# A mixture of experts with its up-projections turned round: weights stationary, 96 token slots streaming

## The chip, the cores and the metric

The kernel runs on one core of one Trainium2 chip. The metric is the device time of one execution in microseconds, given as the median of several runs. TensorE (PE) multiplies a stationary operand, which a weight load (PEld) brings in, with a moving operand that streams through it column by column; results go to PSUM. VectorE (DVE), ScalarE (ACT) and GpSimd (POOL) work beside it, and 16 DMA engines move data from HBM, issued here by SyncE's queue (SP). TensorE's granted clock has two levels, 1.2 and 2.4 GHz; the profile gives it as a share of the upper one.

## What is computed

Two decoder layers over 256 tokens of 1024 channels. Each has a mixer (attention and a short convolution), a feed-forward part and a gated embedding. The feed-forward part is dense in layer 0 and routed in layer 1, which is the part that the change is about:

```python
def moe_swiglu(x, router_w, w1, w3, w2):
    xt = x.reshape(bsz * s_len, d)                       # 256 x 1024
    logits = (xt @ router_w).astype(jnp.float32)         # 8 experts
    top_vals, top_idx = lax.top_k(logits, TOP_K)         # 2 of them for each token
    gates = jax.nn.softmax(top_vals, axis=-1)
    ...
    for e in range(N_EXPERTS):
        out = out + combine[:, e:e + 1] * swiglu(xt, w1[e], w3[e], w2[e])

def swiglu(x, w1, w3, w2):
    return (jax.nn.silu(x @ w1) * (x @ w3)) @ w2         # 1024 -> 3584 -> 1024
```

Its input is `rmsnorm(h, ffn_norm_g)`: h times one factor for each token and one gain for each channel.

## The kernel before

**Precision.** Every large product is made of values in two parts, high and low, both rounded to the type fp32r: x = xh + xl, w = wh + wl. `mm3` (lines 180 to 183) issues three matmuls for each product: low x times high w, high x times low w, and high times high. The weights arrive in fp32; `split` (line 87) makes wh with a ScalarE cast (line 94) and wl with a VectorE subtraction (line 95), in parts of 1024 columns. `plan` lists all weight halves in the order of their use; `weights` and `prepare` keep five split parts (`NPART`) ahead of TensorE, and `loads` keeps the transfers ahead of that.

**Order.** In the routed layer the instructions of TensorE, ScalarE and VectorE run in the order in which the code is written. There is no planner.

**Routing.** `Moe.route` transposes h, makes the router's logits (`logits`, line 717, matmuls of 8 columns), and `choose` ranks them on VectorE, counts each token's slot within its expert with small matmuls (line 746 to 750) and leaves in `pos` the slot of each token. `Gather` builds for a pair of experts a one-hot matrix `sl` of tokens to slots, 128 slots for each expert, and its `step` multiplies the split h (`Parts`, tile `hx`) with it: the result, tile `pg`, holds the tokens of the two experts with channels on the partitions, and `scaled_split` applies the channel gain and makes the two parts of it. The token factor (1/rms) is not yet in it: `slots` brings it to each slot with one-column matmuls (line 820) as `rslot`, together with the transposed matrix `slT` for the way back. An expert that has more than 128 tokens is served by a second pass over all weights (`over`), behind a branch at the end.

**Experts.** Eight experts follow one another, each in 7 blocks of 512 hidden units. `expert_up` makes a block's two up-projections (tile `pe`, one PSUM bank each): the gathered tokens are stationary, 128 slots wide, and the weights stream, 512 columns a matmul; 8 channel blocks times 3 matmuls for each of w1 and w3. Silu with the factor `rslot` (line 843) and the product (line 846) give m with slots on the partitions. `hidden_T` (line 578) transposes m with four matmuls against the identity (line 581) and splits it into `th` and `tl`, which `expert_down` uses as the stationary operand, one block later, against streaming columns of w2 (tile `y`, two banks). `main` writes the order of a block: the four half up-projections, half of the down-projection of the block before, `hidden_T`, the other half. At an expert's end `y_split` and `combine` bring the sums back to the tokens.

The lines of the profile are those of the code below.

Of the kernel before, what the change touches and what calls it, by code (L numbers as in the profile page):

```python
# [16 lines left out]
P = 128  # L17
# [21 lines left out]
# columns of the constant pack  # L39
# [5 lines left out]
def trunk(ctx: ExitStack, tc: tile.TileContext, a, out):  # L45
# [13 lines left out]
    # ---- parameters and constants  # L59
# [11 lines left out]
    onesr = const.tile([P, P], F32R, name="onesr")  # L71
    one1 = const.tile([P, 1], F32, name="one1")
# [7 lines left out]
    # ---- building blocks  # L80
# [52 lines left out]
    def loads(upto):  # L133
        """parts up to that one, loaded"""
# [8 lines left out]
    def prepare(upto, eng=nc.vector):  # L143
        """parts up to that one, split"""
# [45 lines left out]
    class TokenRstd:  # L190
        """1 / rms of each token of h, [P, NT]: part(n) for each half of the channels, then done()"""
# [21 lines left out]
    def x_tiles(raw=False):  # L213
        """two parts of a transposed input; of two that live at a time, one is raw: in weights' slots"""
        return [rawp.tile([P, KD, S], F32R, tag="raw", name=n) if raw else xp.tile([P, KD, S], F32R, tag=n, name=n)
                for n in ("xh", "xl")]

    class Transposed:
        """gain * h over channels, in two parts, and the token factors; step(k) does channels k, k + 1 of 128"""
# [6 lines left out]
        def step(self, k):  # L226
            # a bank for each channel block, so that two engines read at a time
# [78 lines left out]
    # ---- the mixer: attention and short convolution  # L306
    def mixer(l, xt, after):
        """xt: transposed input, whose steps 4 and 6 are still to do where l > 0; after: makes the next one"""
        with tc.tile_pool(name="att", bufs=2) as ap, tc.tile_pool(name="att1", bufs=1) as a1:
# [29 lines left out]
            def v_g():  # L339
                """the values over tokens, and the convolution's input"""  # L340
# [17 lines left out]
            def consts():  # L358
                # of 0 and 1, so the rounding keeps them
# [839 lines left out]
```

## Time and profile before

| | |
|---|---|
| time, median of 3 runs | 1545.15 us (1544.93 to 1545.29) |
| span of the profiled execution | 1541.0 us |
| TensorE busy | 1521.9 us (99%) |
| VectorE busy | 1282.6 us (83%) |
| ScalarE busy | 1096.0 us (71%) |
| chain that ended last | 97% TensorE |
| read from HBM | 443.4 MB, 288 GB/s over the span |
| the experts' stretch | about 522 to 1507 us |

The span is that of one execution under the profiler; the median of the runs is 4.15 us more. Busy time of TensorE is the time in which at least one matmul is under way. A matmul's own duration holds its latency, and matmuls overlap, so the durations of a group add up to more than the time they take; the distance from one start to the next tells the pace. The pages below name a group of instructions by line, engine, operation and "output<-inputs".

### The profile page before, as it was taken

The numbers are of one execution on the slowest core, as the hardware profiler recorded it, in microseconds if no ns is written. First come the engines' busy times: TensorE is split into PE (matmuls) and PEld (weight loads), VectorE is DVE, ScalarE is ACT, GpSimd is POOL, SyncE is SP. The second block draws the span as 40 slices with busy tenths as digits, with TensorE's granted clock in tenths as the row PEclk, the third lists the DMA queues.
The fourth block names the chain that finished last, engine by engine and source line by source line (L and its number), as shares of the span: only waits on it lengthen the run. The fifth ranks groups of instructions, "written<-read, shape, count | busy, mean of one in ns | idle before, by whom it ended". The sixth has DMA issues, their size and how long they took to land.

```text
span 1541.0 us, 19945 instructions
## 1 busy us (share of the span) xinstructions
PE 1521.9 (99%) x7249; PEld 1261.5 (82%) x7249; DVE 1282.6 (83%) x1553; ACT 1096.0 (71%) x1470; POOL 92.7 (6%) x96
## 2 busy tenths in 40 slices
PE   7999999999999999999999999999999999999998
PEld 6888888887888788888888888888888888888886
DVE  7886555556788799899899999999999999999895
ACT  5756444446675687878777778787787887877874
POOL 3430000000243000000000000000000000000000
PEclk9999999999999899999999999999999999999999
DMA  9656554343435699897999998999998899999960
GB/s 359 251 197 241 191 186 176 137 162 111 169 148 203 236 379 371 313 349 288 360 372 375 351 361 328 375 408 378 353 360 331 313 362 368 377 343 338 362 259 30
DMA packets 64043, 445.84 MB, mean 289 GB/s; under 512 B 7104, under 2 KB 9024, under 8 KB 10432
## 3 DMA queue, kind: packets, MB, share of 16 engines
q1 hardware_dynamic: 63936, 444.48, 75.8%
q8 instruction: 59, 0.97, 0.2%
q14 instruction: 48, 0.39, 0.1%
HBM read 443.40 MB, written 1.05 MB: 288 GB/s over the span
## 4 chain that ended last, share of the span: by engine, by line
PE 97%; DVE 1%; DMA 0%; ACT 0%; issue 0%; SPq 0%; POOL 0%; DVEq 0%; ACTq 0%
PE pe L181 13%; PE pe L183 13%; PE pe L182 13%; PE y L183 8%; PE y L182 8%; PE y L181 8%; PE p L183 3%; PE p L182 3%; PE p L181 3%; PE pt L581 2%; PE pu L181 2%; PE pu L182 1%; PE pu L183 1%; PE pj L181 1%; PE pj L183 1%; PE pj L182 1%
## 5 line engine op out<-in xcount | busy, mean ns | idle before, releaser
L95 DVE TENSOR_TENSOR wl<-raw,wh 128x1024 fp32r<-128x1024 f32 (+1 forms) x999 | 1017.6, 1058 | 178.8 <-ACT wh L94 167.3
L94 ACT CAST wh<-raw 128x1024 fp32r<-128x1024 f32 (+1 forms) x1000 | 881.4, 913 | 242.8 <-PE pe L183 78.9
L181 PE MATMUL pe<-wh,xl 128*128 128x512 f32 x896 | 350.6, 391 | 0.0
L183 PE MATMUL pe<-wh,xh 128*128 128x512 f32 x896 | 349.2, 390 | 0.0
L182 PE MATMUL pe<-wl,xh 128*128 128x512 f32 x896 | 348.6, 389 | 0.0
L181 PE MATMUL y<-wh,tl 128*128 128x512 f32 x560 | 226.2, 404 | 0.0
L182 PE MATMUL y<-wl,th 128*128 128x512 f32 x560 | 220.8, 394 | 0.5 <-DVE wl L95 0.5
L183 PE MATMUL y<-wh,th 128*128 128x512 f32 x560 | 220.9, 395 | 0.0
L183 PEld LDWEIGHTS pe<-wh,xh 128*128 128x128 f32 x896 | 168.1, 188 | 36.2
L182 PEld LDWEIGHTS pe<-wl,xh 128*128 128x128 f32 x896 | 168.3, 188 | 35.9 <-DVE wl L95 0.4
L181 PEld LDWEIGHTS pe<-wh,xl 128*128 128x128 f32 x896 | 168.2, 188 | 35.1
L183 PEld LDWEIGHTS y<-wh,th 128*128 128x128 f32 x560 | 105.1, 188 | 25.2
L182 PEld LDWEIGHTS y<-wl,th 128*128 128x128 f32 x560 | 105.3, 188 | 22.7 <-DVE wl L95 1.2
L181 PEld LDWEIGHTS y<-wh,tl 128*128 128x128 f32 x560 | 105.3, 188 | 21.6 <-ACT wh L94 0.2
L181 PE MATMUL p<-wh,xl 128*128 128x512 f32 x224 | 87.8, 392 | 0.0
L183 PE MATMUL p<-wh,xh 128*128 128x512 f32 x224 | 87.3, 390 | 0.0
L182 PE MATMUL p<-wl,xh 128*128 128x512 f32 x224 | 87.2, 389 | 0.0
L585 ACT CAST th<-pt 128x512 fp32r<-128x512 f32 x70 | 40.9, 586 | 41.7 <-PE pt L581 41.7
L95 POOL TENSOR_TENSOR wl<-raw,wh 128x1024 fp32r<-128x1024 f32 x1 | 2.4, 2372 | 990.8 <-ACT wh L94 990.8
L181 PE MATMUL pu<-xh,wl 128*128 128x256 f32 x192 | 56.4, 294 | 0.0
L182 PE MATMUL pu<-xl,wh 128*128 128x256 f32 x192 | 54.2, 282 | 0.0
L183 PE MATMUL pu<-xh,wh 128*128 128x256 f32 x192 | 54.2, 282 | 0.0
(203 smaller groups left out, 1565.4 us busy)
## 6 DMA issues: line engine op xcount, KB each, us to landing
raw<-m_w SPq DMA_DIRECT2D x336, 1024.0 KB, 5.7
raw<-d_w SPq DMA_DIRECT2D x42, 1024.0 KB, 4.8
raw<-w_in SPq DMA_DIRECT2D x22, 1024.0 KB, 6.9
raw<-w_o SPq DMA_DIRECT2D x8, 1024.0 KB, 6.7
raw<-w_g SPq DMA_DIRECT2D x8, 1024.0 KB, 4.8
raw<-w_p SPq DMA_DIRECT2D x2, 1024.0 KB, 4.8
raw<-w_in SPq DMA_DIRECT2D x4, 256.0 KB, 4.4
raw<-w_in SPq DMA_DIRECT2D x2, 512.0 KB, 8.8
```

The lines of the kernel that those rows point to most:

```text
L94: nc.scalar.copy(wh[:, cs], raw[:, cs])
L95: eng.tensor_sub(wl[:, cs], raw[:, cs], wh[:, cs].bitcast(F32))
L181: nc.tensor.matmul(ps, ll, rh, start=start, stop=False)
L182: nc.tensor.matmul(ps, lh, rl, start=False, stop=False)
L183: nc.tensor.matmul(ps, lh, rh, start=False, stop=stop)
L581: nc.tensor.transpose(pt[:, c * P:(c + 1) * P], m[:, c * P:(c + 1) * P], ident)
L585: nc.scalar.copy(th, pv)
```

## The change

- A new constant `CAP = 96` is the number of slots of an expert in a pass. The one-hot matrices, the gathered tokens and the down-projection's stationary operand have 96 slots in place of 128. The branch to the further passes is taken when an expert has more than 96 tokens.
- The gathered tokens are kept as `[channel block, expert, high and low, slot]` in one tile (`Gather.x`).
- `expert_up` has the weights as the stationary operand, 128 hidden columns at a time, and streams the tokens: for each channel block and each of four column blocks q, one matmul of wl with the 96 high slots, and one of wh with the 192 high and low slots, whose low half goes to other columns of the same PSUM bank. An up-projection now has two banks, each with two q's.
- After the last channel block ScalarE copies the low sums to SBUF (tile `lo`), and `fold` adds them to the high sums with an identity matmul. Then come Silu and the product. The result already has hidden units on the partitions, so `hidden_T` isn't called in the experts; `fold(1)` splits it into `th` and `tl`.
- The token factors go into the split of h: `Parts.part` uses `scaled_split` with the factor of each token, which `Route.factors` makes before the choice. Silu and the product have no factor any more, and `slots` no one-column matmuls.
- PSUM: `pe` goes to the four banks of `acc`, `y` to the two of `mm`, the embedding's sums to `tp`. xh and xl of the other stages lie in one tile, `x`. Comments and docstrings are taken out.

```diff
+CAP = 96
 ...
 class Parts:
-            nc.scalar.copy(hh, hn)
-            nc.vector.tensor_sub(hl, hn, hh.bitcast(F32))
+            scaled_split(hh, hl, hn, self.r()[:, t:t + 1])
 ...
 class Route:
+        def factors(self, mp):
+            self.rs.done()
+            self.r = mp.tile([P, NT], F32, tag="rk", name="rk")
+            nc.vector.tensor_copy(self.r, self.rs.r)
 ...
 class Gather:
-            self.sl = mp.tile([P, NT, self.n, P], F32R, tag="sl", name="sl")
+            self.sl = mp.tile([P, NT, self.n, CAP], F32R, tag="sl", name="sl")
 ...
-                nc.tensor.matmul(pt[:, S:S + 1], sl[t], self.rt.r[:, t:t + 1], start=(t == 0), stop=(t == NT - 1))
 ...
 def expert_up
-                st[j] = mm.tile([P, 512], F32, tag="mm", name="pe")
+                st[j] = [acc.tile([P, 512], F32, tag="acc", name="pe") for _ in range(2)]
             w = weights(ws[j](b, hf), 512) if ws else weights(once=True)
             for k in range(4):
                 kk = hf * 4 + k
-                mm3(st[j], g.h[:, kk, ts], g.l[:, kk, ts], *w(k),
-                    start=(kk == 0), stop=(kk == KD - 1))
+                wh, wl = w(k)
+                xk = x(kk)
+                for q in range(4):
+                    ps = st[j][q // 2]
+                    o = q % 2 * CAP
+                    qs = slice(q * P, (q + 1) * P)
+                    nc.tensor.matmul(ps[:, o:o + CAP], wl[:, qs], xk[:, 0, :], start=(kk == 0 and q % 2 == 0),
+                                     stop=False, skip_group_check=True)
+                    nc.tensor.matmul(ps[:, 0:4 * CAP].rearrange("p (a s) -> p a s", a=2)[:, :, o:o + CAP],
+                                     wh[:, qs], xk, start=False, stop=False, skip_group_check=True)
             if hf == 1:
+                st["lo", j] = fp.tile([P, 2, 2 * CAP], F32R, tag="lo", name="lo")
+                for i in range(2):
+                    nc.scalar.copy(st["lo", j][:, i, :], st[j][i][:, 2 * CAP:4 * CAP])
+        def fold(j):
+            for i in range(2):
+                nc.tensor.matmul(st[j][i][:, 0:2 * CAP], late_const["identr"], st["lo", j][:, i, :], start=False, stop=True,
+                                 skip_group_check=True)
 ...
 Moe.route
             rt.logits(1, 1)
+            rt.rs.part(1)
+            rt.factors(self.m1)
+            rt.split.part(0, 0)
+            rt.split.part(0, 1)
+            rt.choose(self.m1, self.m1)
+            g = self.pair(0, rt.split)
             rt.split.part(1, 0)
             rt.split.part(1, 1)
             loads(n + 2 * LOADS[1])
-            rt.choose(self.m1, self.m1)
-            g = self.pair(0, rt.split)
             rt.counts()
-            rt.rs.part(1)
-            rt.rs.done()
 ...
 Moe.main
                     up[2]()
+                    fold(0)
 ...
                         dn[0]()
-                    ht = hidden_T(st["m"], mp) if dn else st["m"]
+                    fold(1)
```

The order of the instructions shows it at three places. First TensorE at the start of an up-projection, the first channel block of the first expert. Before, three matmuls make it (xh and xl are the tokens, wh and wl the weights; behind the arrow the moving operand stands first, the stationary one second):

```order
L181 MATMUL pe_4961<-wh_4664,xl_4874 128x512
L182 MATMUL pe_4961<-wl_4665,xh_4873 128x512
L183 MATMUL pe_4961<-wh_4664,xh_4873 128x512
L181 MATMUL pe_4961<-wh_4664,xl_4874 128x512
L182 MATMUL pe_4961<-wl_4665,xh_4873 128x512
L183 MATMUL pe_4961<-wh_4664,xh_4873 128x512
```

The same place now, where xg are the tokens and the two pe's the two banks:

```order
L858 MATMUL pe_4959<-xg_4869,wl_4662 128x96
L860 MATMUL pe_4959<-xg_4869,wh_4661 128x2x96
L858 MATMUL pe_4959<-xg_4869,wl_4662 128x96
L860 MATMUL pe_4959<-xg_4869,wh_4661 128x2x96
L858 MATMUL pe_4960<-xg_4869,wl_4662 128x96
L860 MATMUL pe_4960<-xg_4869,wh_4661 128x2x96
L858 MATMUL pe_4960<-xg_4869,wl_4662 128x96
L860 MATMUL pe_4960<-xg_4869,wh_4661 128x2x96
```

Three matmuls of 512 columns with two stationary operands of tokens have become eight, of 96 and 192 columns, each with a stationary operand of its own.

Second, TensorE between the two halves of a down-projection (y is its sum). Before, the four transposes of m stand there:

```order
L182 MATMUL y_5148<-wl_5253,th_5174 128x512
L183 MATMUL y_5148<-wh_5252,th_5174 128x512
L581 MATMUL pt_5306<-cst_88,m_5282 128x128 x4
L181 MATMUL y_5147<-wh_5262,tl_5175 128x512
L182 MATMUL y_5147<-wl_5263,th_5174 128x512
```

Now the second fold stands there (lo are the low sums, identr the identity):

```order
L184 MATMUL y_5320<-wl_5252,th_5140 96x512
L185 MATMUL y_5320<-wh_5251,th_5140 96x512
L869 MATMUL pe_5229<-lo_5316,identr_4768 128x192
L869 MATMUL pe_5230<-lo_5316,identr_4768 128x192
L183 MATMUL y_5319<-wh_5276,tl_5141 96x512
L184 MATMUL y_5319<-wl_5277,th_5140 96x512
```

The place of the transposes is taken by two matmuls that wait for ScalarE's copies; another such pair stands between the third and the fourth half of the up-projections.

Third, VectorE in the routing, from the last transposed part of h to the first gather's matrices (sl). Before, h is split without a factor, and the sum of squares (ss) comes last:

```order
L710 COPY hT<-pt 128x4x128
L676 TENSOR_TENSOR hx<-h_97,hx 128x512
L676 TENSOR_TENSOR hx<-h_98,hx 128x512
L726 COPY lg<-plg 128x8
...
L752 COPY pos<-ppos 128x16
L789 TENSOR_SCALAR sl<-cst,pos,sel 128x128 x4
L758 TENSOR_REDUCE cmax<-ppos 128x1
L760 CAST cnt<-cmax 128x1
L205 TENSOR_TENSOR ss<-ss 128x2
L187 TENSOR_SCALAR ms<-ss 128x2
```

Now (rk is the factor of each token, which waits for POOL's power of ms):

```order
L714 COPY hT<-pt 128x4x128
L207 TENSOR_TENSOR ss<-ss 128x2
L189 TENSOR_SCALAR ms<-ss 128x2
L770 COPY rk<-r 128x2
L213 SCALAR_TENSOR_TENSOR hx<-h_97,rk,hx 128x512
L213 SCALAR_TENSOR_TENSOR hx<-h_98,rk,hx 128x512
L730 COPY lg<-plg 128x8
...
L756 COPY pos<-ppos 128x16
L797 TENSOR_SCALAR sl<-cst,pos,sel 128x96 x4
L213 SCALAR_TENSOR_TENSOR hx<-h_97,rk,hx 128x512
L213 SCALAR_TENSOR_TENSOR hx<-h_98,rk,hx 128x512
```

The factor and the split of the first half of the channels stand ahead of the choice now, the split of the second half behind it.

## Rows read from the trace of the kernel before

**Rows 1.** The page: span, busy time, and the chain that ended last by engine.

```profile
span 1541.0 us, 19945 instructions
PE 1521.9 (99%) x7249; PEld 1261.5 (82%) x7249; DVE 1282.6 (83%) x1553; ACT 1096.0 (71%) x1470; POOL 92.7 (6%) x96
PE 97%; DVE 1%; DMA 0%; ACT 0%; issue 0%; SPq 0%; POOL 0%; DVEq 0%; ACTq 0%
```

**Rows 2.** Stretches (us): length, busy PE PEld DVE ACT POOL, clock, DMA share, GB/s.

```profile
550.00:600.00 50.00, 50.00 (x226) 41.06 (x225) 45.78 (x42) 39.66 (x42) 0.00 (x0) 1.00 0.96 371
...
1000.00:1050.00 50.00, 50.00 (x235) 41.26 (x234) 46.74 (x49) 39.09 (x47) 0.00 (x0) 1.00 0.99 398
```

**Rows 3.** The page's costliest groups, up-projections: count, busy us, mean ns.

```profile
L181 PE MATMUL pe<-wh,xl 128*128 128x512 f32 x896 | 350.6, 391 | 0.0
```

**Rows 4.** TensorE in order of time (start, duration): up matmuls, then down matmuls.

```profile
537.32 0.39 PE L182 MATMUL pe<-wl,xh 128*128 128x512 f32 x1
...
545.05 0.39 PE L183 MATMUL pe<-wh,xh 128*128 128x512 f32 x1
...
1504.67 0.39 PE L183 MATMUL y<-wh,th 128*128 128x512 f32 x1
...
1506.77 0.40 PE L183 MATMUL y<-wh,th 128*128 128x512 f32 x1
```

**Rows 5.** TensorE in order of time: the convolution's matmuls of 256 columns.

```profile
100.01 0.28 PE L182 MATMUL pu<-xl,wh 128*128 128x256 f32 x1
...
101.21 0.28 PE L183 MATMUL pu<-xh,wh 128*128 128x256 f32 x1
```

**Rows 6.** Narrow matmuls and their loads in order of time, several merged in a row.

```profile
503.13 1.03 PE L705 MATMUL pt<-cst,h 128*128 128x128 f32 x8
...
506.85 1.53 PEld L717 LDWEIGHTS plg<-rg,hT 128*128 128x128 f32 x13
...
639.02 0.50 PE L820 MATMUL psl<-rk,sl 128*128 128x1 f32 x4
```

**Rows 7.** Weight loads in order of time around the attention's 128-column matmuls in fp32r.

```profile
90.53 0.19 PEld L458 LDWEIGHTS later<-sph,onesr 128*128 128x128 f32 x1
90.64 0.19 PEld L181 LDWEIGHTS pu<-xh,wl 128*128 128x128 f32 x1
90.75 0.19 PEld L182 LDWEIGHTS pu<-xl,wh 128*128 128x128 f32 x1
```

**Rows 8.** Stretches of the attention and the routing; router matmuls: durations, and at the lower clock.

```profile
70.00:80.00 10.00, 10.00 (x70) 8.80 (x68) 9.90 (x18) 7.64 (x16) 5.56 (x6) 1.00 0.32 120
...
511.00:521.20 10.20, 7.29 (x39) 7.14 (x39) 7.46 (x24) 4.95 (x12) 1.61 (x1) 0.50 0.53 206
521.20:531.20 10.00, 10.00 (x51) 8.46 (x51) 6.24 (x14) 7.67 (x13) 0.00 (x0) 1.00 0.84 311
...
L717 PE MATMUL plg<-rg,hT x32: 170/256/361, 506.7 to 511.9; 128*128 128x8 f32 x32
...
511.01 1.21 PE L717 MATMUL plg<-rg,hT 128*128 128x8 f32 x5
```

**Rows 9.** The routing in order of time: ScalarE, VectorE, POOL, TensorE.

```profile
510.96 0.63 ACT L201 ACTIVATE junk<-h 128x512 bf16<-128x512 f32 x1
...
510.24 1.29 DVE L676 TENSOR_TENSOR hx<-h,hx 128x512 fp32r<-128x512 f32 x2
512.26 0.17 DVE L726 COPY lg<-plg 128x8 f32<-128x8 f32 x1 [0.73 <-PE plg L717]
...
516.42 1.61 POOL L188 TENSOR_TENSOR r<-ms,mhalf 128x2 f32<-128x2 f32 x1 [19.24 <-DVE ms L187]
...
515.44 6.63 PE L804 MATMUL pg<-sl,hx 128*128 128x256 f32 x32 [1.00 <-DVE sl L789]
```

**Rows 10.** ScalarE's groups by shape: count, busy us, mean ns.

```profile
L94 ACT CAST wh<-raw 128x1024 fp32r<-128x1024 f32 x679 | 700.4, 1053 | 120.8 <-PE pe L183 78.6 <-PE y L183 30.5 <-DVE wl L95 2.4
...
L824 ACT CAST slT<-psl 128x256 fp32r<-128x256 f32 x8 | 3.0, 379 | 0.0
```

More of the change, by code (lines that the diff above doesn't have):

```diff
@@ L213, in x_tiles @@
     def x_tiles(raw=False):
-        return [rawp.tile([P, KD, S], F32R, tag="raw", name=n) if raw else xp.tile([P, KD, S], F32R, tag=n, name=n)
-                for n in ("xh", "xl")]
+        if raw:
+            return [rawp.tile([P, KD, S], F32R, tag="raw", name=n) for n in ("xh", "xl")]
+        x = xp.tile([P, 2, KD, S], F32R, tag="x", name="x")
+        return [x[:, 0], x[:, 1]]
     class Transposed:
@@ L848, in expert_up @@
-        return [lambda j=j, hf=hf: chunk(j, hf) for j in range(2) for hf in range(2)], st
+                wh, wl = w(k)
[8 more added lines that the diff above has]
+                                     wh[:, qs], xk, start=False, stop=False, skip_group_check=True)
@@ new lines, in chunk @@
+            if hf == 1:
+                st["lo", j] = fp.tile([P, 2, 2 * CAP], F32R, tag="lo", name="lo")
[5 more added lines that the diff above has]
+                                 skip_group_check=True)
+            if j == 0:
+                st["s"] = fp.tile([P, 2, 2 * CAP], F32, tag="s", name="s")
+                for i in range(2):
+                    nc.scalar.activation(st["s"][:, i, :], st[0][i][:, 0:2 * CAP], AF.Silu)
+                return
+            m = fp.tile([P, 4, CAP], F32, tag="m", name="m")
+            mf = m.rearrange("p q s -> p (q s)")
+            for i in range(2):
+                nc.vector.tensor_mul(mf[:, i * 2 * CAP:(i + 1) * 2 * CAP], st[1][i][:, 0:2 * CAP], st["s"][:, i, :])
+            th = fp.tile([P, 4, CAP], F32R, tag="th", name="th")
+            tl = fp.tile([P, 4, CAP], F32R, tag="tl", name="tl")
+            nc.scalar.copy(th, m)
+            nc.vector.tensor_sub(tl, m, th.bitcast(F32))
+            st["t"] = (th, tl)
@@ L850, in expert_down @@
+        return [lambda j=j, hf=hf: chunk(j, hf) for j in range(2) for hf in range(2)], fold, st
     def expert_down(w2, b, ht, ys):
-        st = []
         def chunk(hf):
-            if hf == 0:
-                st.extend(ht())
             if b == 0 and hf == 0:
-                ys.extend(acc.tile([P, 512], F32, tag="acc", name="y") for _ in range(2))
-            th, tl = st
+                ys.extend(mm.tile([P, 512], F32, tag="mm", name="y")[0:CAP, :] for _ in range(2))
+            th, tl = ht
@@ L938, in back @@
                     self.out = [t[:, 0], t[:, 1]]
-                combine(self.out if e else h, self.out, yp[e], sT[e][0], lambda t: rt.gate[:, t, col(e)], n, **where)
+                combine(self.out if e else h, self.out, yp[e], sT[e], lambda t: rt.gate[:, t, col(e)], n, **where)
             for e in range(NE):
+                xg = lambda k, e=e: g[e // 2].x(k, e % 2)
                 for b in range(NB):
-                    up, st = expert_up(None, b, g[e // 2], e % 2, lambda: sT[e][1], mp)
+                    up, fold, st = expert_up(None, b, xg, mp)
                     pe_, pb = (e, b - 1) if b else (e - 1, NB - 1)
-                    dn = expert_down(None, pb, lambda: ht, ys[pe_]) if pe_ >= 0 else ()
+                    dn = expert_down(None, pb, ht, ys[pe_]) if pe_ >= 0 else ()
                     up[0]()
@@ L948, in main @@
                     if more and b == 4:
-                        split = Parts()
+                        split = Parts(lambda: rt.r)
                         split.part(0, 0)
@@ L1014, in over, with embedding @@
                     split.part(n, t)
-            with tc.For_i(0, NE, 1) as e:
-                ce = bass.ds(e, 1)
-                g = Gather(rt, pos2, [ce], mp, split, False)
-                for k in range(0, KD, 2):
-                    g.step(k)
-                slT, rk = g.slots(0)
-                ys, y = [], []
-                w = lambda name: (lambda b, hf: a[name][ce, b, hf].rearrange("o p n -> (o p) n"))
-                for b in range(NB):
-                    up, st = expert_up([w("m_w1"), w("m_w3")], b, g, 0, lambda: rk, mp)
-                    run(up)
-                    ht = hidden_T(st["m"], mp)
-                    run(expert_down(w("m_w2"), b, lambda: ht, ys))
-                for n in range(2):
-                    y_split(ys, y, n)
-                    combine(self.out, self.out, y, slT, lambda t: rt.gate[:, t, ce], n)
-    def embedding(srcs=None):
+            for past in range(CAP, S, CAP):
+                pos2 = self.m1.tile([P, NT, NE], F32, tag="pos2", name="pos2")
+                nc.vector.tensor_single_scalar(pos2, rt.pos, float(-past), op=ALU.add)
+                with tc.For_i(0, NE, 1) as e:
+                    ce = bass.ds(e, 1)
+                    g = Gather(rt, pos2, [ce], mp, split, False)
+                    for k in range(0, KD, 2):
+                        g.step(k)
+                    slT = g.slots(0)
+                    ys, y = [], []
+                    w = lambda name: (lambda b, hf: a[name][ce, b, hf].rearrange("o p n -> (o p) n"))
+                    for b in range(NB):
+                        up, fold, st = expert_up([w("m_w1"), w("m_w3")], b, lambda k: g.x(k, 0), mp)
+                        run(up[0:2])
+                        fold(0)
+                        run(up[2:4])
+                        fold(1)
+                        run(expert_down(w("m_w2"), b, st["t"], ys))
+                    for n in range(2):
+                        y_split(ys, y, n)
+                        combine(self.out, self.out, y, slT, lambda t: rt.gate[:, t, ce], n)
+    def embedding(srcs=None, where=(mm, "mm")):
         st = {}
@@ L1043, in go @@
             ns = slice(n * 512, (n + 1) * 512)
-            ps = mm.tile([P, 512], F32, tag="mm", name="ppp")
+            ps = where[0].tile([P, 512], F32, tag=where[1], name="ppp")
             for k in range(2):
@@ L1089, in trunk @@
         rt = mixer(1, mix, lambda: Route(1))
-        rt.split.part(0, 0)
-        rt.split.part(0, 1)
         with tc.tile_pool(name="moe1", bufs=1) as m1, tc.tile_pool(name="moe2", bufs=2) as mp:
-            prep, pp = embedding()
+            prep, pp = embedding(where=(tp, "t"))
             moe = Moe(rt, m1, mp)
@@ L1109, in trunk @@
             n = nc.values_load(rt.cnt[0:1, 0:1], min_val=0, max_val=S)
-            with tc.If(n > P):
+            with tc.If(n > CAP):
                 moe.over()
```

61 lines of the change are left out of this document (28 added, 33 removed).

## The prediction

> **What bounds the kernel now.** I read the page first: TensorE is busy for 99% of the 1541.0 us span, and the chain that ended last is 97% PE [rows 1]. The table of stretches says the same of the experts (from 522 to 1507 us): 50.00 of 50 us are TensorE's, at the full clock, while VectorE has 45.78 and ScalarE 39.66, and the loads run at 371 to 398 GB/s [rows 2]. So a stretch of TensorE that is made longer shows one for one in the time; one made shorter does so only until VectorE or the loads are the bound. Half of the experts' time is their up-projections: three lines of 896 matmuls [rows 3], 2688 in 56 blocks (8 experts of 7), 48 a block.
>
> The busy times of [rows 3] must not be added up, since matmuls overlap (3 x 350 us would be more than the stretch holds). What counts is the distance between starts. From the matmul at 537.32 to the one at 545.05 there are 34 steps: 7.73 / 34 = **227.4 ns** for each up matmul of 512 columns; the down matmuls take (1506.77 - 1504.67) / 9 = **233 ns** [rows 4]. A block is thus 48 x 0.2274 + 24 x 0.233 + four transposes of 0.11, or 16.9 us, which fits some three blocks (226 matmuls, 76 a block) in 50 us.
>
> **How the price of a narrow matmul is read.** The change makes the weights stationary. Every matmul then brings its own weight load of 128 columns, and streams only 96 or 192 columns. Old stretches with few columns show what that costs. With 256 columns, ten steps take 1.20 us, 120 ns each [rows 5]. From 256 to 512 columns the step grows by 107 ns, so a column costs 0.42 ns and about 12 ns are fixed; 96 and 192 columns alone would be 52 and 93 ns. But the step does not go on falling: eight transposes of 128 columns take 1.03 us, of which the last one's own 0.27 is latency, so (1.03 - 0.27) / 7 = 109 ns; the router's matmuls of 8 columns have 13 weight loads in 1.53 us, (1.53 - 0.19) / 12 = 112 ns [rows 6]. So some 110 ns is the floor of a weight load of 128 four-byte columns, whatever is streamed. The same holds in the type used here: around the attention's 128-column matmul the loads start at 90.53, 90.64 and 90.75, 110 ns apart [rows 7]. Both 96 and 192 columns lie under that floor.
>
> **The change, part by part.**
>
> *Up-projection.* Per block and matrix, 8 k's x 4 blocks of 128 hidden columns x 2 matmuls = 64 in place of 24. Over 56 blocks and two matrices that is 7168 in place of 2688. Removed: 2688 x 0.2275 = 611.5 us. Added: between 7168 x 0.1085 = 778 us (the transposes' step) and 7168 x 0.120 = 860 us (the step at 256 columns, if its extra 10 ns come with any pair of load and stream). I take 111 ns, between the 110 of the same type and the 112 of the router: 795.6 us. The sum is **+184 us**, with ends at +166 and +249. All of it is on TensorE, which has no idle time to take it. The columns do fall, from 1536 to 1152 per k, but they are no longer what is waited for.
>
> *Fold and transposes.* Four identity matmuls a block (192 columns, one load each) come, 224 x 0.111 = 24.9 us; the four transposes of m go, 224 x 0.1085 = 24.3 us. Net +0.6. The first fold waits for two ScalarE copies of 192 columns; the nearest row is a copy of 256 columns at 0.38 us, so some 0.8 us, and with a weight cast of 1.05 us ahead of it 1.9 us [rows 10]. It is covered by the half up-projection that TensorE does meanwhile (32 x 0.111 = 3.6 us), the second by half a down-projection (12 x 0.233 = 2.8 us). Behind a late fold all of TensorE would queue; without that cover up to 1 us x 112 = 112 us would show, which I leave out because the cover is longer. The products after the fold feed the down-projection one block later.
>
> *Removed work.* The token factor of each slot goes: four one-column matmuls an expert, 0.50 us of which some 0.13 are the last one's latency [rows 6], 8 x 0.37 = -3.0 us. The gathers have 192 in place of 256 columns: 128 x (0.120 - 0.111) = -1.1 us. Silu and the product work on 384 in place of 512 columns, and the extra copies are some 1.5 us of ScalarE a block; neither engine is the bound of a 20 us block. The loads need 6.3 MB in 20 us instead of 17, and become easier.
>
> *Factors in the split of h.* This sits at the one place where TensorE waits for VectorE: between the router and the first gather. Before, VectorE went from the last logits (512.26) to the gather's start (515.44), 3.2 us, with h already split [rows 9]. Now the sums of squares, POOL's power and the split of the first half come ahead of the choice. The last squares take ScalarE 1.5 us (0.63 and a read, twice) from 509.7 on, so 511.2; two short VectorE steps, 0.35; POOL's power, 1.61 in this place, and a short copy; then ScalarE's two halves at some 0.6 each (as the squares of 512 columns) and VectorE's last at 0.65 [rows 9]. That ends near 515.3, and the 3.2 us follow: the gather starts at 518.5, 3.1 us later, and VectorE's second pair ahead of the first evictions may cost another 0.5. I take **+3.6 us**, all idle on TensorE; it can't be below nothing, as the chain only gets longer, and with the second pair in full (1.3) it is 4.4. The other three gathers' splits lie under the experts. Nothing else is moved past; the loads keep their queue.
>
> Sum: 184.1 + 0.6 - 3.0 - 1.1 + 3.6 = **+184.2 us**. The profiled run of 1541.0 would become 1725.2; the median stands 4.15 us above that span, and 1545.15 + 184.2 = **1729 us**.
>
> **The rivals.**
>
> *The weight loads hide (faster).* If a load of the next weights ran fully under the stream, the steps would be 52 + 93 ns a pair: 3584 x 0.145 = 520 us, 92 us saved. The loads of the experts' 6.3 MB a block at the best 398 GB/s need 15.8 us of the 16.9, so at most 56 x 1.05 = 59 us come through: 1486 us. The point from which the change wins is 611.5 / 7168 = 85 ns a matmul. Against it: with streams of 8, 128 and 256 columns nothing that loads 128 four-byte columns stepped under 108 ns [rows 5 to 7]. For it: none of these is a long stretch of just this pattern. The Trainium skill, "TensorE: Matmul & The Clock Gate", section "Back-to-back issue gap", has about 81 ns for sustained load and matmul pairs at 128 columns; by that the up-projections would be 7168 x 0.081 = 581 us and the kernel 30 us faster. [rows 6] show 109 ns at 128 columns, so the trace does not agree for this type.
>
> *The clock stays low at first.* The granted clock fell to half (1.2 GHz) at 511 us, after some 3 us of the router's 8-column matmuls, transposes and a wait; it came back to 2.4 at 521.2, after the gather had streamed 256 columns without a gap [rows 8]. At the lower level the router's steps were (1.21 - 0.36) / 4 = 213 ns [rows 8]. In the changed kernel the gather streams 192 columns per load and the up-projection 96 and 192, so the first wide matmuls are the down-projections in the second block. If the clock comes back only there, two blocks run at 213 ns: 256 x 0.102 = 26 us, and 2.5 more for folds and the first down matmuls: **1758 us**.
>
> *Every matmul has the 120 ns of the 256-column rows.* +249 us instead of +184: **1794 us**.
>
> *The clock falls in every block.* If it falls during each block's up-projections, half or all of the 128 up matmuls take 213 ns: 56 x 6.5 to 56 x 13 us more, 2100 to 2450 us. Against it: the clock held through the attention, where narrow matmuls mix with wide ones [rows 8], and after every block come 5.6 us of wide ones.
>
> *It does something else.* An expert with over 96 tokens would start the second pass over all weights. The reference's own inputs give at most 74 tokens to an expert, so I give that no chance.
>
> **How the numbers follow.** Forecast 45%; low clock at first 27%; 120 ns 14%; clock falling in each block 6%; hidden loads 6%; anything else 2%. The range of 1705 to 1797 holds the first three with the lower end of the weight load (1711, and a few us of margin); outside it lie the last three and some 5% of the first ones' tails, so about 8 in 10 are inside. What a measurement tells from no change here is about 0.2%, 3 us. Faster: the hidden loads, 6%. Same: 1%. Slower: 93%.
>
> **What would show it.** In the changed profile the up matmuls should step by 109 to 112 ns whether they stream 96 or 192 columns, a pair 222 ns; TensorE should stay at 50 of 50 us, a block should be 20.3 us, VectorE's share should fall to some 75% and the loads to some 310 GB/s. The two folds should wait for nothing. The gather should start 3 to 4 us later after the last logits. A pair at 145 ns would say that loads hide, at 240 that the fixed part counts, at 426 that the clock is down: the clock row tells which. I am wrong in the sign if the step is under 85 ns, and wrong in the mechanism if TensorE sits idle in the experts, at a fold or for wl.

## The result, and the profile after

The changed kernel takes **1730.13 us** (median of 4 runs, 1729.64 to 1731.33) against 1545.04 beside it: ratio 1.1202, 95% interval [1.1186, 1.1218]. The forecast was 1729, the range 1705 to 1797, slower with 93%.

The page of the changed kernel: span, busy time, the chain by engine, and the up-projections' groups (count, busy us, mean ns).

```profile
span 1728.1 us, 29164 instructions
PE 1703.6 (99%) x11697; PEld 1522.3 (88%) x11697; DVE 1283.4 (74%) x1609; ACT 1141.3 (66%) x1742; POOL 92.2 (5%) x97
PE 97%; DVE 1%; ACT 0%; POOL 0%; issue 0%; DMA 0%; SPq 0%; DVEq 0%; ACTq 0%
L860 PE MATMUL pe<-xg,wh 128*128 128x192 f32 x3584 | 812.4, 319 | 0.0
L858 PE MATMUL pe<-xg,wl 128*128 128x96 f32 x3584 | 800.2, 230 | 0.0
```

As in [rows 1], TensorE holds 99% of the span and 97% of the chain; the span is 187.1 us longer, and VectorE's busy time is the same 1283 us, now 74% of it. Stretches of the routing and of the experts (length, busy PE PEld DVE ACT POOL, clock, DMA share, GB/s):

```profile
511.00:521.20 10.20, 4.36 (x29) 3.73 (x26) 6.77 (x22) 5.84 (x12) 0.70 (x1) 0.58 0.62 262
521.20:531.20 10.00, 9.79 (x67) 9.83 (x68) 6.92 (x19) 4.47 (x10) 0.00 (x0) 0.74 0.57 206
550.00:600.00 50.00, 50.00 (x388) 45.96 (x388) 37.26 (x36) 35.72 (x49) 0.00 (x0) 1.00 0.83 308
1000.00:1050.00 50.00, 50.00 (x400) 46.73 (x398) 39.52 (x39) 35.97 (x50) 0.00 (x0) 1.00 0.74 268
```

Against [rows 2], TensorE is still at 50.00 of 50 us and at the full clock, VectorE has fallen from 46 to 38 us and the loads from 371 and 398 GB/s to 308 and 268: both run behind a slower TensorE. TensorE in order of time (start, duration) shows the slower step itself:

```profile
999.73 0.32 PE L860 MATMUL pe<-xg,wh 128*128 128x192 f32 x1
999.89 0.23 PE L858 MATMUL pe<-xg,wl 128*128 128x96 f32 x1
999.96 0.32 PE L860 MATMUL pe<-xg,wh 128*128 128x192 f32 x1
...
1001.29 0.32 PE L860 MATMUL pe<-xg,wh 128*128 128x192 f32 x1
```

From 999.73 to 1001.29 there are seven pairs: 223 ns a pair, **111.5 ns** a matmul, where [rows 4] have 227.4 for one of 512 columns. The mean over the experts is 223.0. The recorded starts split a pair into 66 and 157 ns; what does that is open, and only the sum is used below.

By place these 187 us are: 1.8 before the routing (the granted clock was 0.50 from 17.8 to 21.2 us, which it was not in the trace before), 3.2 in the routing (first router matmul to first up matmul, 15.16 and 18.38), 180.9 in the experts (first up to last down matmul: 984.9 and 1165.8), 1.1 behind them. The routing in order of time:

```profile
511.58 2.58 PE L721 MATMUL plg<-rg,hT 128*128 128x8 f32 x16 [0.24 <-ACT hT L712]
...
513.37 0.70 POOL L190 TENSOR_TENSOR r<-ms,mhalf 128x2 f32<-128x2 f32 x1 [14.36 <-DVE ms L189]
...
515.06 1.42 DVE L213 SCALAR_TENSOR_TENSOR hx<-h,rk,hx 128x512 fp32r<-128x512 f32 x2 [0.79 <-ACT hx L212]
...
518.26 0.19 PE L750 MATMUL ppos<-selb,bits 128*128 128x8 bf16 x1 [4.10 <-DVE selb L745]
...
519.52 1.14 PE L821 MATMUL pg<-sl,hx 128*128 128x192 f32 x4 [0.96 <-DVE sl L797]
519.77 1.41 DVE L213 SCALAR_TENSOR_TENSOR hx<-h,rk,hx 128x512 fp32r<-128x512 f32 x2
...
521.40 5.70 PE L821 MATMUL pg<-sl,hx 128*128 128x192 f32 x28 [0.74 <-DVE cmax L762]
526.94 0.23 PE L858 MATMUL pe<-xg,wl 128*128 128x96 f32 x1
```

From the end of the router's matmuls to the gather's start VectorE had 3.2 us in [rows 9]. Now it splits h first (515.06), and TensorE waits 4.10 us for the choice alone. Then the gather starts (519.52), and after four matmuls stops again until 521.40: its second sum needs the PSUM tile of `ppos`, whose counts VectorE reads (cmax) only behind the second split (519.77, 1.41 us).

### The profile page after: what moved, and what is told of

It is laid out like the page before. It is cut to its first block, busy times and chain, and to the rows that moved or that the text cites. A ratio compares the mean times of both kernels' runs of the same rounds, so it can differ in the third digit from the quotient of the medians.

```text
span 1728.1 us, 29164 instructions
## 1 busy us (share of the span) xinstructions
PE 1703.6 (99%) x11697; PEld 1522.3 (88%) x11697; DVE 1283.4 (74%) x1609; ACT 1141.3 (66%) x1742; POOL 92.2 (5%) x97
## 4 chain that ended last, share of the span: by engine, by line
PE 97%; DVE 1%; ACT 0%; POOL 0%; issue 0%; DMA 0%; SPq 0%; DVEq 0%; ACTq 0%
PE pe L860 32%; PE pe L858 14%; PE y L185 7%; PE y L183 7%; PE y L184 7%; PE p L184 3%; PE p L185 3%; PE p L183 3%; PE pu L183 2%; PE pe L869 1%; PE pu L184 1%; PE pu L185 1%; PE pj L183 1%; PE pj L184 1%; PE pj L185 1%; PE pg L821 1%
## 5 line engine op out<-in xcount | busy, mean ns | idle before, releaser
L860 PE MATMUL pe<-xg,wh 128*128 128x192 f32 x3584 | 812.4, 319 | 0.0
L858 PE MATMUL pe<-xg,wl 128*128 128x96 f32 x3584 | 800.2, 230 | 0.0
L858 PEld LDWEIGHTS pe<-xg,wl 128*128 128x128 f32 x3584 | 687.8, 192 | 4.2
L860 PEld LDWEIGHTS pe<-xg,wh 128*128 128x128 f32 x3584 | 687.9, 192 | 3.1
L183 PE MATMUL y<-wh,tl 128*96 128x512 f32 (+1 forms) x560 | 221.2, 395 | 0.0
L185 PE MATMUL y<-wh,th 128*96 128x512 f32 (+1 forms) x560 | 220.4, 393 | 0.0
L184 PE MATMUL y<-wl,th 128*96 128x512 f32 (+1 forms) x560 | 219.9, 393 | 0.5 <-DVE wl L97 0.5
L184 PEld LDWEIGHTS y<-wl,th 128*96 128x96 f32 (+1 forms) x560 | 93.4, 167 | 28.9 <-DVE wl L97 1.2
L183 PEld LDWEIGHTS y<-wh,tl 128*96 128x96 f32 (+1 forms) x560 | 93.7, 167 | 28.3 <-ACT wh L96 0.2
L183 PE MATMUL p<-wh,x 128*128 128x512 f32 x224 | 87.8, 392 | 0.0
L185 PE MATMUL p<-wh,x 128*128 128x512 f32 x224 | 87.3, 390 | 0.0
```

What stands on the lines that cost most here:

```text
L183: nc.tensor.matmul(ps, ll, rh, start=start, stop=False)
L184: nc.tensor.matmul(ps, lh, rl, start=False, stop=False)
L185: nc.tensor.matmul(ps, lh, rh, start=False, stop=stop)
L858: nc.tensor.matmul(ps[:, o:o + CAP], wl[:, qs], xk[:, 0, :], start=(kk == 0 and q % 2 == 0), stop=False, skip_group_check=True)
L860: nc.tensor.matmul(ps[:, 0:4 * CAP].rearrange("p (a s) -> p a s", a=2)[:, :, o:o + CAP], wh[:, qs], xk, start=False, stop=False, skip_grou ...
```

## The experiments

The question was not whether the loads set the step, but in what way: what a load costs, what hides under it, and whether the clock and the other engines let a cheaper pattern through. Means of steps below are from start to start over the experts' stretch of each trace.

**A shorter load of half the matmuls.** `e1_bf16low` (to make room it, e5, e9 and e11 also keep one buffer in place of two for the tiles `s` and `m`):

```diff
+        if lo:
+            wl = wl.bitcast(BF16)[:, 0:w]
...
+                nc.gpsimd.tensor_copy(self.b[:, k + kk], x[:, :, 0, :].bitcast(F32))
...
-                    nc.tensor.matmul(ps[:, o:o + CAP], wl[:, qs], xk[:, 0, :], ...
+                    nc.tensor.matmul(ps[:, o:o + CAP], wl[:, qs], xb(kk), ...
```

> The changed kernel, but the low part of the up-projections' weights is written as bf16, and multiplied with a bf16 copy of the gathered tokens' high part (POOL makes the copy). The high part keeps its fp32r loads. Theory (the time of an up-projection is the time to load 128 four-byte stationary columns, about 111 ns, once per matmul): the bf16 loads are short (in the trace of before five of them start 0.03 us apart in the routing), so a pair falls from 223 ns to between 141 (the fp32r load and a short one) and 163 (the fp32r load and the 52 ns of a 96-column stream). 3584 pairs: 215 to 294 us less than the changed kernel, 1436 to 1515 us, and not under some 1485 where the weight transfers become the bound. Rival (a fixed price for each matmul, whatever its load): no less than 1730. Rival (columns streamed, or the way the sums are written, set the step): 1730, since the columns are the same.

Measured: 1704.14 us, ratio 1.1034 [1.1016, 1.1053]. A miss: the pair fell only from 223.0 to 215.7 ns.

```profile
900.03 0.22 PE L867 MATMUL pe<-xb,wl 128*128 128x96 bf16 x1
900.07 0.33 PE L869 MATMUL pe<-xg,wh 128*128 128x192 f32 x1
900.24 0.22 PE L867 MATMUL pe<-xb,wl 128*128 128x96 bf16 x1
```

So my theory in its first form, that the pair is the sum of two loads, fell. Either a load does not get shorter in bf16, or a matmul has a fixed price, or the saving was covered by something else.

**Half the columns of each load.** `e3_half` loads 64 of 128 hidden columns from the second channel block on, and leaves the other half's sums out:

```diff
+                    nw = P if kk == 0 else 64
+                    qs = slice(q * P, q * P + nw)
```

> The changed kernel, but from the second channel block on an up matmul loads only the first 64 of its 128 hidden columns: half of the hidden units get only the first channel block's share, so the result lacks that work. The number of matmuls and the columns streamed are as in the changed kernel; 7 of 8 loads have half the columns. Theory (load floor, proportional to the columns loaded): such a load takes about 56 ns, so the streams of 96 and 192 columns become the bound, 52 + 93 = 145 to 150 ns a pair in place of 223: 3136 x 0.075 = 235 us less, about 1495 us. Rival (a fixed price for each matmul): 1730 us, unchanged.

Measured: 1517.53 us, 0.9825 [0.9809, 0.9842], and a pair of 146 ns (the median; 0.15 us in these rows):

```profile
899.90 0.21 PE L859 MATMUL pe<-xg,wl 128*64 128x96 f32 x1
899.95 0.26 PE L861 MATMUL pe<-xg,wh 128*64 128x192 f32 x1
900.05 0.21 PE L859 MATMUL pe<-xg,wl 128*64 128x96 f32 x1
```

A fixed price for each matmul is refuted: the streams are the same and the pair falls by 77 ns, to what the prediction worked out from the columns alone, 52 + 93 = 145 ns. One rival is left by this run, since half the loaded columns also means half the rows written to PSUM; e5 below writes all of them. The Trainium skill, "TensorE: Matmul & The Clock Gate", section "LDWEIGHTS (loading the stationary operand)", makes a load proportional to its columns; by its formula an estimate is 107 ns for 128 and 53 for 64. This case agrees, 111 for 128, and at 64 the load no longer shows. The total missed by 22 us. Part of that is in the waits of e3's TensorE (us, times, longest), which now waits for VectorE's `wl`:

```profile
PE pe L859 <- DVE wl L97: 11.6, 13, 1.5
```

So VectorE begins to hold TensorE up; it is one of the two next bounds that the prediction named for a faster TensorE. What the rest of the 22 us is was not followed up.

**Fewer slots.** `e2_cap64` has 64 slots and leaves out the tokens beyond (`CAP = 64`, the further pass only above 128).

> The changed kernel with 64 slots for each expert in place of 96, and without the further pass: tokens past an expert's 64th are left out, so a part of the routed sum is missing. The up matmuls stream 64 and 128 columns in place of 96 and 192, with the same number of weight loads. Theory (load floor): the step stays at 111 ns, the time at 1727 to 1731 us. Rival (columns streamed set the step): 96 columns less a pair at 0.42 ns, 40 ns x 3584 = 144 us less, 1586 us.

Measured: 2293.87 us, 1.4842 [1.4812, 1.4871], which neither the theory nor its rival had. Stretches of e2 (columns as above):

```profile
589.30:596.10 6.80, 6.80 (x49) 5.56 (x48) 5.47 (x8) 4.41 (x5) 0.00 (x0) 1.00 0.58 177
596.10:620.00 23.90, 23.90 (x107) 22.49 (x107) 9.36 (x8) 8.73 (x14) 0.00 (x0) 0.50 0.58 208
```

TensorE in order of time in these two stretches, at the full and at the lower clock:

```profile
594.10 0.25 PE L858 MATMUL pe<-xg,wl 128*128 128x64 f32 x1
594.18 0.31 PE L860 MATMUL pe<-xg,wh 128*128 128x128 f32 x1
594.33 0.25 PE L858 MATMUL pe<-xg,wl 128*128 128x64 f32 x1
...
599.96 0.36 PE L858 MATMUL pe<-xg,wl 128*128 128x64 f32 x1
600.13 0.45 PE L860 MATMUL pe<-xg,wh 128*128 128x128 f32 x1
600.38 0.36 PE L858 MATMUL pe<-xg,wl 128*128 128x64 f32 x1
```

At the full clock the pair is 221 ns on the mean, next to 223 with 96 slots, so the load holds it. But the granted clock falls to 0.50 again and again, 54 times in the 56 blocks, although TensorE is busy in 6.80 of 6.80 us before the fall shown and in 23.90 of 23.90 behind it, and the pair is then 426. This is the rival "the clock falls in every block", with the price it was given (2100 to 2450), in a kernel with two thirds of the columns.

**Order and type apart.** A theory that fits e2 at the full clock, e3 and, but for 12 ns a pair, e1: a step lasts as long as the longer of *the present stream* and *the next load*. In e1 the short load lay under the long stream of 192 columns, which hid it; that its pair is 215.7 ns and not the 111 + 93 = 204 of the theory stays open. `e5_low_first` keeps e1's types and does the four low matmuls of a channel block first; `e6_order_alone` has this order with the types of the changed kernel:

```diff
                 for q in range(4):
+                    nc.tensor.matmul(st[j][q // 2][:, q % 2 * CAP:q % 2 * CAP + CAP], wl[:, q * P:(q + 1) * P], xb(kk), ...
+                for q in range(4):
                     ...
                     nc.tensor.matmul(ps[:, 0:4 * CAP]..., wh[:, qs], xk, ...
```

> The low part of the up weights in bf16 as in e1_bf16low, and the order within a channel block turned: the four matmuls of the low part (96 columns) first, then the four of the high part (192 columns). Theory now held: a step lasts as long as the longer of two things, the present stream and the load of the next weights, plus some nanoseconds; in e1 the short load lay under the long stream, which hid the saving (111 + 93 = 204, measured 215.7). With the low parts in a row, three short loads meet short streams (about 52 ns each), one long load meets a short stream (111), three long loads meet long streams (111), one short load meets a long stream (93): 3 x 52 + 111 + 333 + 93 = 693 ns per channel block, 173 a pair instead of 215.7, so 3584 x 0.043 = 153 us less than e1's 1704: about 1551 us. Rival 1, every matmul has a fixed price whatever it loads: pair 216 to 223, 1704 to 1730 us. Rival 2, VectorE or ScalarE takes over: pair 173 between waits, with PE idle in every block, 1570 to 1620 us.

> The order of e5 (four low matmuls, then four high) with the types of the changed kernel (every load 128 columns of four bytes). Theory: each load of 111 ns is longer than either stream, so the order changes nothing: the pair stays 214 to 223 ns, 1700 to 1730 us, most likely 1725. Rival, the alternation of the two shapes costs something of its own (the 9 ns by which e1's pair was over its sum): pair 205, 1665 us. If e6 were as fast as e5, the type of the low part would not matter and the theory would fall.

Measured: e5 1547.35 us, 1.0016 [1.0006, 1.0026]; e6 1731.1 us, 1.1201 [1.1177, 1.1225]. First e5, then e6, a channel block each from one row of low matmuls to the next:

```profile
547.90 0.35 PE L863 MATMUL pe<-xb,wl 128*128 128x96 bf16 x4
548.07 0.68 PE L869 MATMUL pe<-xg,wh 128*128 128x192 f32 x4
548.59 0.35 PE L863 MATMUL pe<-xb,wl 128*128 128x96 bf16 x4
```

```profile
899.96 0.56 PE L854 MATMUL pe<-xg,wl 128*128 128x96 f32 x4
900.36 0.65 PE L860 MATMUL pe<-xg,wh 128*128 128x192 f32 x4
900.85 0.56 PE L854 MATMUL pe<-xg,wl 128*128 128x96 f32 x4
```

0.69 and 0.89 us: the theory said 0.693 for e5 and no change for e6. The order alone is worth nothing, the short load alone 26 us, both together 183 us. In a row, the low matmuls of e5 step by 43 ns from the second one on, so the bf16 load is no longer than that. It is also less than the 52 ns that the theory took for these steps, so its sum fits by terms that are off both ways. And e5 writes the same sums to PSUM as the changed kernel, so the writing is not what held the low matmuls there.

**More columns.** `e7_128_slots` (`CAP = 128`, and one buffer for `m`).

> The changed kernel with 128 slots in place of 96: streams of 128 and 256 columns. Theory (longer of next load and present stream): the low matmul stays at the load's 111 ns, the high one rises from the load's 111 to the stream's 120: pair 231 to 235 in place of 223, 3584 x 8 to 12 ns = +29 to +43 us, folds and gathers +3: 1762 to 1776 us. Rival 1, a fixed price per matmul: 223, 1733 us. Rival 2, the columns are paid on top of the load (0.42 ns each): 96 more columns a pair, +40 ns, 1875 us.

Measured: 1760.49 us, 1.1398 [1.1378, 1.1419].

```profile
909.84 0.23 PE L858 MATMUL pe<-xg,wl 128*128 128x128 f32 x1
909.90 0.33 PE L860 MATMUL pe<-xg,wh 128*128 128x256 f32 x1
910.07 0.22 PE L858 MATMUL pe<-xg,wl 128*128 128x128 f32 x1
```

The mean pair is 231.5 ns, 8.5 more than with 96 slots: what the theory gives the high matmul, whose stream is now longer than the load. The recorded starts can't say which of the two has grown. Below the load columns are free, as the theory has it: at the full clock the pair is 221 ns with 64 slots (e2), 222.6 with 80 (e10, below) and 223.0 with 96.

**The rest of the change without the turn.** `e4_tokens_still` takes the up-projection back to stationary tokens (96 slots), with transposes of m in place of the folds, and leaves everything else; `e8_tokens_still_128` the same with 128 slots.

```diff
-                for q in range(4):
-                    ...
+                mm3(st[j], xk[:, 0, :], xk[:, 1, :], *w(k), start=(kk == 0), stop=(kk == KD - 1))
```

> The change without its first part: tokens are stationary again (96 slots) and the weights stream 512 columns; m is transposed as before. The 96 slots, the token factors in the split of h, the order of the routing and the PSUM pools are as in the changed kernel. Theory: all but 184 us of the added time belongs to the orientation, and the rest of the change is the routing's +3.2 us, -3.0 for the one-column matmuls and -1.1 for the gathers: 1542 to 1547 us. Rival (the slots, the pools or the order of the routing carry a part of the added time): more than 1550 us.

> As e4 (tokens stationary again, the rest of the change kept), but with 128 slots. In e4 the step of an up matmul was 235.2 ns against 227.4 in the kernel before, 2688 x 7.8 ns = 21 us, not foreseen. Theory, the stationary operand of 96 columns costs it: 227.4 again, transposes back to 108 ns (+6 us): 1544 to 1550 us. Rival, the layout or the PSUM banks cost it (tokens in one tile, the sums in other banks): 235 stays, 1565 to 1570 us.

Measured: e4 1560.69 us, 1.0102 [1.0086, 1.0119], a miss; e8 1540.61 us, 0.9970 [0.9957, 0.9983]. Two up matmuls of e4, two of e8 in order of time:

```profile
900.25 0.40 PE L183 MATMUL pe<-wh,xg 128*96 128x512 f32 x1
900.48 0.40 PE L184 MATMUL pe<-wl,xg 128*96 128x512 f32 x1
```

```profile
899.80 0.39 PE L184 MATMUL pe<-wl,xg 128*128 128x512 f32 x1
900.03 0.39 PE L185 MATMUL pe<-wh,xg 128*128 128x512 f32 x1
```

On the mean, 235 ns in e4 and 227 in e8: with 96 slots these matmuls of 512 columns are 8 ns slower than with 128, 2688 times, 22 us. Why is open, and it is no rule for a stationary operand of 96 columns: the down matmuls of the changed kernel have one too and step by 231 ns, next to 230 in e7 with 128.

So the turn of the up-projection is read from two pairs of kernels with the same slots: with 96, e4 and the changed kernel are 169 us apart; with 128, e8 and e7 are 220 us apart. The rest of the change, without the turn, is a gain of 4.5 us with 128 slots (e8) and a loss of 16 us with 96 (e4, for its slow matmuls). In the changed kernel, whose up-projections no longer have the slow matmuls of e4, the whole loss is the turn's.

**Fewer columns, and the granted clock.** `e10_80_slots` is the changed kernel with `CAP = 80`, `e9_low_first_80` e5 with it. In `e11_wide_gather` e9's gathers alone go back to 128 slots:

```diff
-            self.sl = mp.tile([P, NT, self.n, CAP], F32R, tag="sl", name="sl")
+            self.sl = mp.tile([P, NT, self.n, P], F32R, tag="sl", name="sl")
...
-                             pts[kk].rearrange("p (i s) -> p i s", s=CAP), par[:, gc:gc + 1])
+                             pts[kk].rearrange("p (i s) -> p i s", s=P)[:, :, 0:CAP], par[:, gc:gc + 1])
```

> e5_low_first with 80 slots (no expert has more than 74 tokens): streams of 80 columns of the low part and 160 of the high. Theory (a step is the longer of present stream and next load): the high matmuls keep the load's 111 ns, the three low ones fall by 16 x 0.42 = 6.7 ns each, as does the last high one's stream (32 columns, up to 13 ns, if the short load does not hold it): 20 to 33 ns less per channel block, 896 blocks of them: 18 to 30 us off e5's 1547: 1517 to 1529 us, less what VectorE (45 of 50 us busy in e5's experts) lets through, so most likely 1528. Rival 1, the low matmuls are already at the bf16 load and not at their stream: nothing, 1545. Rival 2, the granted clock falls in the up-projections as with 64 slots: over 1800 us.

> The changed kernel with 80 slots: streams of 80 and 160 columns, every load 128 columns of four bytes. By the theory of loads alone it is the changed kernel: pair 221 to 223 ns, 1725 to 1732 us. What it is run for is the clock: with 96 slots the granted clock stayed at 1.00 through the experts, with 64 slots it fell to 0.5 for most of each round and 2294 us came out. If the clock holds with 80: 1728; if it falls in a share of the blocks, between 1750 and 2250; I expect it to hold in most blocks, 6 in 10.

> e9_low_first_80 with the gathers alone back at 128 slots an expert (256 columns a matmul in place of 160); the up-projections still stream 80 and 160. In e9 and in e10 the granted clock was 0.5 from 515 to 573 us and from 516 to 591, the gather over at 529; in the kernel before it came back during the gather of 256 columns, in the changed kernel at the end of its gather of 192. Theory: the gather's columns bring it back; it is low for 10 to 14 us, the 44 us at the lower clock in the experts go, which at about half speed are 20 us; the gathers cost 1 us more: 1519 to 1524 us, faster than both kernels. Rival: the up-projections themselves keep it low until the wide matmuls of the down-projections, whatever the gather did: 1540 us as e9.

Measured: e9 1540.51 us, 0.9998 [0.9969, 1.0026]; e10 1757.73 us, 1.1379 [1.1360, 1.1399]; e11 **1519.60 us, 0.9840 [0.9827, 0.9854]**. Stretches of e10, then of e9, then of e11:

```profile
530.00:591.40 61.40, 61.23 (x277) 59.05 (x277) 23.27 (x29) 23.13 (x34) 0.00 (x0) 0.50 0.46 160
591.40:641.00 49.60, 49.60 (x384) 44.88 (x383) 37.98 (x39) 34.27 (x45) 0.00 (x0) 1.00 0.82 293
```

```profile
529.00:549.00 20.00, 20.00 (x133) 19.70 (x133) 9.92 (x16) 10.38 (x15) 0.53 (x2) 0.50 0.65 231
549.00:573.00 24.00, 24.00 (x143) 22.23 (x143) 12.56 (x13) 11.93 (x19) 0.00 (x0) 0.50 0.57 200
573.00:623.00 50.00, 50.00 (x474) 43.24 (x473) 44.87 (x46) 42.13 (x58) 0.00 (x0) 1.00 0.91 347
```

```profile
529.00:549.00 20.00, 19.01 (x232) 18.84 (x232) 16.47 (x21) 17.61 (x28) 0.00 (x0) 1.00 0.83 308
549.00:573.00 24.00, 24.00 (x209) 19.88 (x209) 21.64 (x24) 19.57 (x28) 0.00 (x0) 1.00 0.98 381
...
1000.00:1200.00 200.00, 199.52 (x1888) 172.06 (x1888) 186.90 (x197) 164.66 (x236) 0.00 (x0) 1.00 0.96 375
```

With 80 slots the low clock of the routing goes on: in e10 until 591.4 and in e9 until 573.1, each time when the first wide down matmuls had begun (586.5 and 570.0). After that it stays at 1.00 for the rest of the experts. e10 is 27.6 us slower than the changed kernel for it. In e11 the gather streams 256 columns a matmul, the clock is back by 529 though the up-projections are e9's, and 20.9 us go. The mean granted clock tells the two apart in every execution: 0.992 to 0.993 in e11's five, 0.962 to 0.979 in e9's twelve. Since nothing but the gathers differs, the rival that the up-projections keep the clock low whatever the gather did is refuted for this kernel. e11 is below both kernels, 1.6% below the one before; in its experts VectorE has 186.90 of 200 us, so it is near the next bound. The part of the range that e9 missed is this low clock, not its step: a channel block took 0.64 us there, where the theory's saving of 20 to 33 ns would have left at least 0.65.

**The routing by itself.** `e12_no_factor_in_split` leaves the token factor out of the experts' inputs, so that h is split as before; the order in `Moe.route` goes back with it, with both halves split early and the factor behind the choice:

```diff
-            scaled_split(hh, hl, hn, self.r()[:, t:t + 1])
+            nc.scalar.copy(hh, hn)
+            nc.vector.tensor_sub(hl, hn, hh.bitcast(F32))
```

> The changed kernel with the split of h as in the kernel before (no token factor in it, both halves split early, the factor's power behind the choice). It leaves the token factor of the experts' inputs out. Theory: the routing's term of the sum stands by itself, 3.2 us from the first router matmul to the first up matmul, 1.1 of it the second wait of TensorE in the gather: 1726 to 1727.5 us, ratio to the changed kernel 0.998, and the trace has 15.2 us in place of 18.4 from the first router matmul to the first up matmul. Rival: the longer routing is not the factors' but the clock's (13.7 us at half in place of 10.2): 18 us stay, 1730 us.

Measured: 1726.21 us, 1.1174 [1.1159, 1.1189].

```profile
517.11 0.19 PE L751 MATMUL ppos<-selb,bits 128*128 128x8 bf16 x1 [1.92 <-DVE selb L746]
...
518.37 5.74 PE L822 MATMUL pg<-sl,hx 128*128 128x192 f32 x32 [0.96 <-DVE sl L798]
```

The wait for the choice is 1.92 us, and the second one is gone, since the counts now follow the choice at once; 3.9 us less than the changed kernel. The stretch is 13.7 us, less than the 15.2 expected. The low clock lasted 6.8 us here, 13.7 in the changed kernel and 10.2 in the kernel before, whose wait for the choice was also 1.92 us. So it differs apart from that wait, and the run does not fully part the theory from its rival: how much of the routing's term is the factors' and how much the clock's stays open.

## Why the prediction was right, by its steps

**The bound** was read rightly: TensorE stayed at 50 of 50 us, and the 180.9 us in the experts are close to the sum without the routing (180.6).

**The up-projection.** 7168 matmuls were taken at 111 ns, between the transposes' 108.5 and 120; they took 111.5. From start to start they hold 799.5 us of TensorE, where the 2688 before held 612.8: a term of +186.7 instead of +184.1. The rows that carried it were those of narrow matmuls [rows 6] and the loads 110 ns apart [rows 7]. The 81 ns a pair of load and matmul that the prediction set against them, from the Trainium skill, "TensorE: Matmul & The Clock Gate", section "Back-to-back issue gap", did not come with 128 four-byte columns: the changed kernel, e6 and e2 at the full clock have 110 to 112. The sum came nearer than this term because of one that it had left out: the down matmuls step by 231 ns instead of 233. Together with the transposes or the folds next to them they hold 335.2 us in place of 337.8, which is 2.6 less where the sum had 0.6 more. That these errors cancel is luck.

**Folds, one-column matmuls, gathers.** Two folds start 0.10 us apart, next to 0.11 taken; none of them is among the waits of TensorE, as predicted. The gather's step fell from 0.120 to 0.112, as taken, and the one-column matmuls that went were worth 3.6 us, not 3.0.

**The routing.** +3.2 in place of +3.6, but with parts off on both sides: POOL's power took 0.70 us, not 1.61; VectorE's two splits 1.42, not one behind ScalarE's; the second wait 1.15 us from start to start (0.74 of it idle), not 0.5, and for the counts' tile rather than for an eviction. The gather started 5.7 us behind the last router matmul in place of 3.6, that is 2.1 later and not 3 to 4: so this sign that the prediction named did not come, and its sum held by luck, because the second wait was larger. How much of the +3.2 is the clock's is open (e12). To read the counts ahead of the second split would take that wait away; it was not tried.

**The rivals.** Hidden loads: refuted for this pattern, and e5 shows what the price to be beaten (85 ns) needs: 0.69 us a channel block is 86 ns a matmul, and 1547 us is level with before. 120 ns each: not with 192 columns, but with 256 (e7) the pair is what 111.5 and 120 give. Low clock at first: it did not come in the four executions of the changed kernel; in the profiled one the clock was back at 526.4, as the gather of 192 columns ended. With 80 slots it came as described and cost 27.6 us, where 28.5 was worked out. That 96 slots are safe from it is not shown: one execution of e6, which has the changed kernel's loads and columns and is left out of its ratio, took 1758.27 us at a mean granted clock of 0.977, where the other three have 0.993 to 0.994; no trace of it was kept, so its cause is open. So 27% was no mistake. The clock falling in every block: not with 96, but with 64. That rival was priced rightly and given 6%, on rows of an attention whose narrow matmuls stand among wide ones.

## What to carry to other kernels

Price a matmul by the longer of its stream and the next operand's load, not by its columns: whoever makes the wide operand stationary gives away every column that lies under the load. If loads must be many, order them so that short loads meet short streams. And before a stream is made narrower, look at the granted clock in the stretch before it: here the cut from 96 to 80 columns saved nothing under the load and cost 27.6 us at the low clock.

## What was not expected of the hardware

- A bf16 load of 128 columns takes at most 43 ns, a four-byte one 111, and yet bf16 low parts alone won 7 of a pair's 223 ns; only the order let more through, 172 ns a pair (e1, e5).
- The granted clock fell to 0.50 while TensorE was busy: 54 times in e2's experts, with streams of 64 and 128 columns under loads of 128. From 700 to 2200 us TensorE was busy for 1499.8 of 1500 us there, and the mean granted clock was 0.66.
- With 96 slots in place of 128 the up matmuls of 512 columns step by 235 ns in place of 227 (e4, e8), while the down matmuls, with the same 96 stationary columns, step by 231. Why is open.
